# Linear attention within chunks: 32x32 blocks alone instead of 128-token score tiles

## The chip, the cores and the metric

One core of one Trainium2 chip. The metric is the device time of one execution, in microseconds (us); the kernel before was run three times, and one more execution was profiled.

## The reference, cut to what matters

The program is two networks one after the other, two layers each; the second one's layers hold the part that is changed. There, 512 tokens (256 of a context, 256 latent) are mixed by three mixers side by side: a gated linear attention with 6 heads (keys of 32, values of 64), a short convolution and a neighbourhood attention. The linear attention runs over the tokens in both directions, in chunks. In one direction, with decays accumulated into `q_dec` and `k_inv`:

```python
a = jnp.einsum('bnihk,bnjhk->bnhij', q_dec, k_inv)      # scores, within a chunk
a = jnp.where(causal, a, 0.0)
o_intra = jnp.einsum('bnhij,bnjhv->bnihv', a, v)
def step(s, xs):
    qd, ke, vv, dec = xs
    o = jnp.einsum('bihk,bhkv->bihv', qd, s)            # from the state before the chunk
    s = s * dec[..., None] + jnp.einsum('bjhk,bjhv->bhkv', ke, vv)
    return s, o
```

The two directions are added, each head is normalised by the root of its mean square, and the result is multiplied by a gate. All is fp32. The kernel takes chunks of 32 tokens (`GC`).

## The kernel before

The large products (`mtile`, `tokmajor`, `wtile`) form the main line: weights come in units of 128x1024, are split by ScalarE and VectorE into a high and a low part (`unit`), and each product is three matmuls of 128x128 against 256 to 512 columns (`mm3`, L388 to L390). The mixers are generators. The main line hands out a budget at each `tick`, also within a product (`inner`), and a generator spends what it yields; `until` runs the generators without any main product until one has finished. A scheduler then settles each engine's order when the program is built: it may take a main matmul of later program order ahead of one whose operands are not there. Inside `manual_schedule(engines={PE})` TensorE's instructions keep their order.

In PSUM, three banks (`mm`) belong to the main line, one (`ada`) to the modulation, and four (`ax`) to all else: the generators `gla` (linear attention) and `na` (neighbourhood attention) share these four.

`gla` prepares `Q[a]` and `K[a]` for a = 0 (forward, four heads), 1 (backward, four heads) and 2 (the last two heads, both directions); 32 partitions are one head. It then runs the chain of states `U` over the chunks (32x32 matmuls `ax<-bigA,bigD`), and then its last loop, one step for each 128 tokens: four steps in the first layer, two in the second. A step has for each r of four heads

- three matmuls of the scores, 32 rows by 128 columns of K against 128 columns of Q (`ax<-slG,slG`): the scores of 128 tokens with 128 tokens, of which only the four 32x32 blocks on the diagonal count;
- two masked copies and a multiplication on VectorE (L1595, L1596, L405), which write `AT[r]`, zero outside the blocks;
- two matmuls of `AT[r]`, 128x128, with 64 columns of values (`ax<-bigA,AT`), and up to twelve 32x32 matmuls of `Q2` with the state `U` (`ax<-gU,gq`), all added up in one bank, in a fixed order;
- a copy of this bank into `ot` by ScalarE.

The step ends with an addition on VectorE, a square on ScalarE, sums on VectorE, a power on GpSimd (`grr`, L519), a scaling on VectorE, three transposes on TensorE (L1644) and the product with the gate. After the first layer's short convolution `until` waits for `gla`; the next products of the main line are the queries and keys of the neighbourhood attention (`nqk(1)`, `nqk(2)`).

Of the kernel before, what the change touches and what calls it, by code (L numbers as in the profile page):

```python
# [10 lines left out]
U32 = mybir.dt.uint32  # L11
AF = mybir.ActivationFunctionType
ALU = mybir.AluOpType
# [26 lines left out]
ADA_MIX = range(16, 40)  # L40
MIX_PACE = 1.8
LAG = 2
GY = 300
GZ = 1500
SQP = (False, True)
GACT = True
# [14 lines left out]
GC = 32  # L61
# [34 lines left out]
def head_cols(base, heads):  # L96
# [3 lines left out]
C_VAL, C_GLU, C_GATE, P_IN, P_GATE, Q, K, V, A_GATE, QI, KI, WI = (  # L100
    0, 256, 512, 768, 1024, 1280, 1792, 2304, 2816, 3328, 3584, 3648)
# [178 lines left out]
def consts2():  # L280
    p = np.arange(128)
    f = p % 16
    inv = (np.float32(10000.0) ** (-np.arange(8, dtype=np.float32) / np.float32(8))).astype(np.float32)
    t = np.arange(T)
    pos = np.where((f < 8)[:, None], (t // 64)[None, :], (t % 64)[None, :]).astype(np.float32)
    ang = pos * inv[f % 8][:, None]
    sign = np.where(p % 32 < 16, -1.0, 1.0).astype(np.float32)[:, None]
    c = GC
    nch = 128 // c
    mats = []  # L290
    for back in range(2):
        m = np.zeros((128, 128 + 2 * nch))
        for i in range(128):
            c0 = i // c * c
            if not back:
                mid = c0 + c // 2 - 1
                m[mid + 1 : i + 1, i] = 1
                m[i + 1 : mid + 1, i] = -1
            else:
                mid = c0 + c // 2  # L300
                m[i:mid, i] = 1
                m[mid:i, i] = -1
        for k in range(nch):
            m[k * c : k * c + c // 2, 128 + 2 * k] = 1
            m[k * c + c // 2 : k * c + c, 129 + 2 * k] = 1
        mats.append(m / 16.0)
    j, i = np.arange(128)[:, None], np.arange(128)[None, :]
    same = j // c == i // c
    mf, mb, mbs = same & (j <= i), same & (j >= i), same & (j > i)
    sgn = np.where(p < 64, 1.0, -1.0)[:, None]  # L310
    qsc = np.where(p < 64, 32.0**-0.5, 1.0)[:, None]
    return np.concatenate(
        [np.cos(ang), np.sin(ang) * sign] + mats + [mf, mf, mb, mbs, 1.0 + np.eye(128), sgn, qsc], 1).astype(np.float32)


def consts0():
# [36 lines left out]
class Prog:  # L353
# [775 lines left out]
    def block2(s):  # L1129
        nc, A = s.nc, s.A  # L1130
        with ExitStack() as c:
            s.tmp = c.enter_context(s.tc.tile_pool(name="b2", bufs=1))
            c2 = s.t([128, A["c2"].shape[1]], "c2")
            nc.scalar.dma_start(c2, A["c2"])
            nch = 128 // GC
            w = 128 + 2 * nch
            s.cos, s.sin = c2[:, 0:256], c2[:, 256:512]
            s.gm = [c2[:, 512 + i * w : 512 + (i + 1) * w] for i in range(2)]
            o = 512 + 2 * w
            s.gmask, s.gdiag = c2[:, o : o + 512].bitcast(U32), c2[:, o + 512 : o + 640]  # L1140
            s.sgn, s.qsc = c2[:, o + 640 : o + 641], c2[:, o + 641 : o + 642]
            s.AT = [s.t([128, 256], f"AT{r}") for r in range(4)]
            for r in range(4):
                nc.gpsimd.memset(s.AT[r], 0.0)
            for i in range(DEPTH):
                s.layer2(i)

            R = s.spread(s.rstd_cols(s.st["ps"][:, 0:2], 2, 1.0 / D), 2)
            for k in range(KT):
                y = s.x2[:, k, T:]  # L1150
                s.stt(y, y, s.sp2[0]["fin"][:, k : k + 1], R[:, :T], ALU.mult, ALU.mult)
                if k % 2:
                    q = nc.sync if k % 4 == 1 else nc.scalar
                    q.dma_start(s.out[:, k - 1 : k + 1], s.x2[:, k - 1 : k + 1, T:])
# [306 lines left out]
    def gla(s, i, P, gw, v, glr, qk, both, c0, st8):  # L1461
        nc = s.nc
        mx = s.mx
        nch = 128 // GC
        NC = 4 * nch
# [4 lines left out]
        ps = s.bank()  # L1470
# [4 lines left out]
        for t in range(4):  # L1475
            ps = s.bank()
# [11 lines left out]
        Q = [s.sl("G") for _ in range(3)]  # L1488
        K = [s.sl("G") for _ in range(3)]
        w = 128 + 2 * nch  # L1490
        Dp = []
        for a, (d, off, dup) in enumerate([(0, 0, False), (1, 192, False), (0, 128, True), (1, 320, True)]):
            H = s.t([128, 4, 2 * nch], "gH", 2, pool=mx)
            for tp in ((0, 2) if d == 0 else (0, 2)):
                ps = s.bank()
                for t in (tp, tp + 1):
                    o = slice((t - tp) * w, (t - tp + 1) * w)
# [7 lines left out]
                c = slice(tp * 128, tp * 128 + 256)  # L1505
# [10 lines left out]
                else:  # L1516
                    x = s.t([128, T], "gx", 2, pool=mx)
                    s.a(vw(x), pv[:, :, 0:128], AF.Exp, scale=s.sgn)
                    o = slice(d * 64, d * 64 + 64)
# [27 lines left out]
            yield 0  # L1547

        U = s.t([128, 3, NC, 64], "gU", 1, pool=mx)
        fw = list(range(NC))  # L1550
        bw = list(range(NC // 2))[::-1] + list(range(NC // 2, NC))[::-1]
        sel = [(0, 0, slice(0, 128)), (2, 0, slice(0, 64)), (1, 1, slice(0, 128)), (2, 1, slice(64, 128))]
# [26 lines left out]
        st8["chain"] = True  # L1579
        while "r" not in st8:  # L1580
            yield None
        first = {0: 0, 1: NC // 2 - 1}
        out = s.big([128, 3, 512], "B")
        for t in tts:
            tc = slice(t * 128, t * 128 + 128)

            for r in range(4):
                ps = s.bank()
                rows = slice(r * 32, r * 32 + 32)
                for o, a in enumerate((0, 2, 1)):  # L1590
                    s.mm(ps[:, o * 128 : o * 128 + 128], K[a][rows, tc], Q[a][rows, tc])

                m0 = 0 if r < 2 else 128
                A2 = s.AT[r]
                nc.vector.copy_predicated(A2, s.gmask[:, m0 : m0 + 256], ps[:, :256])  # L1595
                nc.vector.copy_predicated(A2[:, 0:128], s.gmask[:, 384:512], ps[:, 256:384])  # L1596
                s.tt(A2[:, 0:128], A2[:, 0:128], s.gdiag, ALU.mult)
                yield 460

            Q2 = []  # L1600
            ch = slice(t * nch, t * nch + nch)
            for a in range(3):
                q2 = s.t([128, 128], "gq2", 3, pool=mx)
                for d, pr in ([(a, slice(0, 128))] if a < 2 else [(0, slice(0, 64)), (1, slice(64, 128))]):
                    Da = Dp[a] if a < 2 else Dp[2 + d]
                    f0 = first[d]
                    s.tt(q2[pr].rearrange("p (c x) -> p c x", x=GC),
                         Q[a][pr, tc].rearrange("p (c x) -> p c x", x=GC),
                         Da[pr, ch].unsqueeze(2).to_broadcast([pr.stop - pr.start, nch, GC]), ALU.mult)
                Q2.append(q2)  # L1610
            yield 600
            ot = s.sl("O", (128, 2, 4, 64))
            for r in range(4):
                with s.tc.manual_schedule(engines={mybir.EngineType.PE}):
                    ps = s.bank()
                    rows = slice(r * 32, r * 32 + 32)
                    h2 = 4 + r % 2
                    ops = []
                    ops.append((ps[:, 0:64], s.AT[r][:, 0:128], v[:, t, r * 64 : r * 64 + 64]))
                    ops.append((ps[:, 64:128], s.AT[r][:, 128:256], v[:, t, h2 * 64 : h2 * 64 + 64]))  # L1620
                    for a, d, col in [(0, 0, 0), (1, 1, 0), (2, 0 if r < 2 else 1, 64)]:
                        for c in range(nch):
                            ck = t * nch + c
                            pc = slice(c * GC, c * GC + GC)
                            if ck != first[d]:
                                ops.append((ps[pc, col : col + 64], Q2[a][rows, pc], U[rows, a, ck]))
                    for q, (o_, l, rh) in enumerate(ops):
                        s.mm(o_, l, rh, q == 0, q == len(ops) - 1, skip_group_check=True)
                s.a(ot[:, :, r], ps[:, :128].rearrange("p (c d) -> p c d", c=2), AF.Copy)
                if GY:  # L1630
                    yield GY
            s.tt(ot[:, 1, 0:2], ot[:, 1, 0:2], ot[:, 1, 2:4], ALU.add)
            of = ot.rearrange("p a b d -> p (a b d)")[:, 0:384]
            o3 = of.rearrange("p (h d) -> p h d", d=64)
            sq = s.sl("O", (128, 384))
            s.a(sq, of, AF.Square)
            ss = s.t([128, 6], "gss", 2, pool=mx)
            nc.vector.tensor_reduce(ss, sq.rearrange("p (h d) -> p h d", d=64), AX.X, ALU.add)
            yield 700
            rr = s.rstd_cols(ss, 6, 1.0 / 64, "gr")  # L1640
            s.tt(o3, o3, rr.unsqueeze(2).to_broadcast([128, 6, 64]), ALU.mult)
            ps = s.bank()
            for j in range(3):
                nc.tensor.transpose(ps[:, j * 128 : j * 128 + 128], of[:, j * 128 : j * 128 + 128], s.ident)  # L1644
            s.stt(out[:, :, tc], ps[:, :384].rearrange("p (j t) -> p j t", j=3), P["glag"], st8["r"][:, :, tc],
                  ALU.mult, ALU.mult)
            yield GZ
# [127 lines left out]
```

## Time and profile before

| | us |
|---|---|
| three runs | 1440.94, 1443.52, 1445.94 (median 1443.52) |
| profiled execution | 1444.92 |
| its span | 1443.1 |

In the profile PE is TensorE's matmuls, PEld its weight loads, DVE VectorE, ACT ScalarE, POOL GpSimd, SP the queue that starts most transfers. A row of instructions names line, engine, operation, what is written from what, partitions x elements, and how many (x). A matmul's form begins with rows*columns of its stationary operand. An fp32 matmul leaves two records, a matmul of the split main line one. Matmuls overlap, so the distance from start to start tells more than the length of one; the last number of a granted clock is a share of 2.4 GHz.

### The profile page before, as it was taken

The page shows a single profiled execution, that of the slowest core. Times are in us where ns is not written, and L with a number is a line of the kernel's source. Part 1 is how long each engine was busy: PE and PEld are TensorE (multiplying, and loading weights), DVE is VectorE, ACT ScalarE, POOL GpSimd, SP SyncE. Part 2 cuts the span into 40 slices and gives each one's busy share as a digit, 9 for nine tenths or more (in the row PEclk, how much of TensorE's full clock was granted, in tenths as well). Part 3 has the DMA queues.
Part 4 walks back from the last instruction along what each step waited for, and adds up shares of the span by engine and source line. Part 5 has one row for each costly group of instructions (what it writes and reads, how often), then busy time and mean ns, then how long its engine had stood idle before and what let it go on. Part 6 is the DMA issues. An engine that isn't in the chain of part 4 may idle for free.

```text
span 1443.1 us, 25346 instructions
## 1 busy us (share of the span) xinstructions
PE 1388.4 (96%) x9914; PEld 1188.0 (82%) x9914; DVE 1134.6 (79%) x2430; ACT 671.9 (47%) x1234; POOL 68.4 (5%) x92
## 2 busy tenths in 40 slices
PE   8999899998999999998999999999899999999997
PEld 7878899788978777678888888888788887999997
DVE  6998679997879666897788877888678556798794
ACT  4446555465753241545443312443145346565562
POOL 0000000000200001003000000001200000100001
PEclk9999899998999998999999999999999999999998
DMA  7973356334543432332444564557732232366662
GB/s 263 330 250 118 103 170 201 125 104 130 194 148 116 132 100 73 117 114 89 133 144 132 160 191 146 174 177 251 229 115 89 89 97 88 116 212 197 183 198 74
DMA packets 63903, 219.03 MB, mean 152 GB/s; under 512 B 7270, under 2 KB 12328, under 8 KB 63528
## 3 DMA queue, kind: packets, MB, share of 16 engines
q1 hardware_dynamic: 58368, 209.22, 45.8%
q10 hardware_dynamic: 5416, 8.20, 1.7%
q8 instruction: 78, 1.28, 0.4%
q14 instruction: 41, 0.34, 0.1%
HBM read 216.34 MB, written 1.05 MB: 151 GB/s over the span
## 4 chain that ended last, share of the span: by engine, by line
PE 73%; DVE 11%; issue 6%; DMA 4%; ACT 3%; POOL 2%; ACTq 0%; POOLq 0%; DVEq 0%; SPq 0%
PE mm L388 20%; PE mm L389 20%; PE mm L390 19%; PE ax L385 9%; DVE hl L449 3%; DMA wada<-in_wadaT_dram 2%; PE mm L385 1%; DMA raw<-in_units_dram 1%; PE ax L1728 1%; PE ada L385 1%; POOL sqa L537 1%; DVE xx L396 1%; DVE wada L683 1%; DMA crow<-in_crow_dram 1%; ACT hl L441 1%
## 5 line engine op out<-in xcount | busy, mean ns | idle before, releaser
L388 PE MATMUL mm<-xx,hl 128*128 128x256 f32 (+1 forms) x1720 | 557.5, 326 | 5.5 <-ACT xx L414 2.0
L390 PE MATMUL mm<-xx,hl 128*128 128x256 f32 (+1 forms) x1720 | 547.1, 319 | 1.6 <-DVE hl L449 1.5
L389 PE MATMUL mm<-xx,hl 128*128 128x256 f32 (+1 forms) x1720 | 547.6, 319 | 0.0
L441 ACT ACTIVATE hl<-raw 128x1024 fp32r<-128x1024 f32 x286 | 301.3, 1055 | 186.8 <-PE mm L390 152.4
L449 DVE TENSOR_TENSOR hl<-raw,hl 128x1024 fp32r<-128x1024 f32 x286 | 348.9, 1221 | 49.3 <-ACT hl L441 47.6
L388 PEld LDWEIGHTS mm<-xx,hl 128*128 128x128 f32 x1720 | 325.6, 190 | 51.8 <-issue 17.9
L390 PEld LDWEIGHTS mm<-xx,hl 128*128 128x128 f32 x1720 | 325.9, 190 | 30.6 <-DVE hl L449 3.2
L389 PEld LDWEIGHTS mm<-xx,hl 128*128 128x128 f32 x1720 | 326.5, 190 | 28.4 <-issue 4.9
L396 DVE SCALAR_TENSOR_TENSOR y<-mm,sp,y 128x255 f32<-128x255 f32 (+1 forms) x184 | 109.0, 595 | 30.9 <-ACT y L409 29.6
L389 PE MATMUL mm<-hid,hl 128*128 128x256 f32 (+1 forms) x374 | 124.2, 332 | 0.0
L388 PE MATMUL mm<-hid,hl 128*128 128x256 f32 (+1 forms) x374 | 124.2, 332 | 0.0
L390 PE MATMUL mm<-hid,hl 128*128 128x256 f32 (+1 forms) x374 | 124.1, 332 | 0.0
L683 DVE CUSTOM_DVE_ANT_0 wada<-wada,crow,sp 128x1024 f32<-128x1024 f32 x80 | 102.9, 1292 | 13.6 <-DMA wada<-in_wadaT_dram 13.2
L409 ACT ACTIVATE y<-mm,sp 128x256 f32<-128x256 f32 (+1 forms) x92 | 60.5, 658 | 97.9 <-PE mm L390 97.8
L390 PEld LDWEIGHTS mm<-hid,hl 128*128 128x128 f32 x374 | 71.9, 192 | 7.1
L388 PEld LDWEIGHTS mm<-hid,hl 128*128 128x128 f32 x374 | 71.8, 192 | 7.1
L389 PEld LDWEIGHTS mm<-hid,hl 128*128 128x128 f32 x374 | 71.8, 192 | 7.1
L389 PE MATMUL mm<-hl,xx 128*128 128x416 f32 (+3 forms) x192 | 65.9, 346 | 2.5 <-DVE hl L449 2.5
L396 DVE SCALAR_TENSOR_TENSOR x<-mm,mod,x 128x256 f32<-128x256 f32 x96 | 43.6, 479 | 30.2 <-PE mm L390 30.1
L537 POOL TENSOR_TENSOR sqa<-sqa,sq 128x256 f32<-128x256 f32 x36 | 35.3, 987 | 675.7 <-ACT sq L409 674.8
L388 PE MATMUL mm<-hl,xx 128*128 128x416 f32 (+3 forms) x192 | 65.9, 349 | 0.2 <-ACT hl L441 0.2
L390 PE MATMUL mm<-hl,xx 128*128 128x416 f32 (+3 forms) x192 | 65.6, 344 | 0.0
(278 smaller groups left out, 1691.0 us busy)
## 6 DMA issues: line engine op xcount, KB each, us to landing
raw<-in_units_dram SPq DMA_DIRECT2D x296, 512.0 KB, 3.8
wada<-in_wadaT_dram SPq DMA_DIRECT2D x80, 512.0 KB, 3.5
wada<-in_wada_dram SPq DMA_DIRECT2D x16, 512.0 KB, 6.2
nab<-in_nab_dram ACTq DMA_DIRECT2D x12, 192.0 KB, 3.4
crow<-in_crow_dram SPq DMA_DIRECT2D x2, 1024.0 KB, 7.4
x<-in_xT_dram SPq DMA_DIRECT2D x4, 256.0 KB, 5.9
x<-in_ctxT_dram ACTq DMA_DIRECT2D x1, 1024.0 KB, 11.9
c<-in_c_dram ACTq DMA_DIRECT2D x1, 928.0 KB, 5.9
```

The costliest lines, as they stand in the source:

```text
L385: return s.nc.tensor.matmul(out, lhsT, rhs, start=start, stop=stop, **kw)
L388: s.nc.tensor.matmul(out, l[0], r[0], start=start, stop=False)
L389: s.nc.tensor.matmul(out, l[0], r[1], start=False, stop=False)
L390: s.nc.tensor.matmul(out, l[1], r[0], start=False, stop=stop)
L396: s.nc.vector.scalar_tensor_tensor(out, a, sc, b, op0, op1)
L409: s.nc.scalar.activation(out, in_, func, bias=bias, scale=scale)
L441: a = nc.scalar.activation(hl[:, 0], raw, AF.Copy)
L449: b = nc.vector.tensor_sub(hl[:, 1], raw, hl[:, 0].bitcast(F32))
L537: (eng or s.nc.vector).tensor_tensor(st["acc"], st["acc"], sq, ALU.add)
L683: s.pin(nc.vector.tensor_tensor_reduce(out=w, in0=w, in1=c[:, j], scale=1.0, scalar=bias[:, m : m + 1], op0=ALU.mult, op1=ALU.add, accum_o ...
L1728: nc.tensor.transpose(pt[:, kt * 128 : kt * 128 + 128], L[j][:, kt * 128 : kt * 128 + 128], s.ident)
```

## The change

The scores are computed by 32x32 blocks alone, each into its 32 partitions and 32 columns of a bank, two heads at once in two banks, TensorE's order kept. ScalarE copies each head's 96 columns into `pk`, and after all four heads VectorE masks them at once into `AT[t % 2]`, which now has 4 x 64 columns. Scores times values are 32x32 matmuls too, per chunk, into one bank `px` for all heads of the step, which VectorE adds to `of` after the last head; the state matmuls keep a bank for each head. They now run over the first chunk of each direction too, whose state is cleared to zero by GpSimd. The yields of a step change (`GY` and others), and the masks among the constants shrink to 32 columns.

```diff
-GY = 300
+GY = 200
...
-            s.AT = [s.t([128, 256], f"AT{r}") for r in range(4)]
-            for r in range(4):
+            s.AT = [s.t([128, 4, 2 * GC], f"AT{r}") for r in range(2)]
+            for r in range(2):
                 nc.gpsimd.memset(s.AT[r], 0.0)
...
+        first = {0: 0, 1: NC // 2 - 1}
+        for a, d, pr in [(0, 0, slice(0, 128)), (1, 1, slice(0, 128)), (2, 0, slice(0, 64)), (2, 1, slice(64, 128))]:
+            nc.gpsimd.memset(U[pr, a, first[d]], 0.0)
...
-            for r in range(4):
-                ps = s.bank()
-                rows = slice(r * 32, r * 32 + 32)
-                for o, a in enumerate((0, 2, 1)):
-                    s.mm(ps[:, o * 128 : o * 128 + 128], K[a][rows, tc], Q[a][rows, tc])
-
-                m0 = 0 if r < 2 else 128
-                A2 = s.AT[r]
-                nc.vector.copy_predicated(A2, s.gmask[:, m0 : m0 + 256], ps[:, :256])
-                nc.vector.copy_predicated(A2[:, 0:128], s.gmask[:, 384:512], ps[:, 256:384])
-                s.tt(A2[:, 0:128], A2[:, 0:128], s.gdiag, ALU.mult)
-                yield 460
+            pk = s.t([128, 4, 3 * GC], "gpk", 1, pool=mx)
+            for r0 in (0, 2):
+                bk = [s.bank(), s.bank()]
+                with s.tc.manual_schedule(engines={mybir.EngineType.PE}):
+                    for o, a in enumerate((0, 2, 1)):
+                        for c in range(nch):
+                            for r in (r0, r0 + 1):
+                                rows = slice(r * 32, r * 32 + 32)
+                                pc = slice(t * 128 + c * GC, t * 128 + c * GC + GC)
+                                s.mm(bk[r - r0][c * GC : c * GC + GC, o * GC : o * GC + GC], K[a][rows, pc], Q[a][rows, pc])
+                for r in (r0, r0 + 1):
+                    s.a(pk[:, r], bk[r - r0][:, : 3 * GC], AF.Copy)
+                yield 300
+
+            A2 = s.AT[t % 2]
+            nc.vector.copy_predicated(A2, s.gmask, pk[:, :, 0 : 2 * GC])
+            nc.vector.copy_predicated(A2[:, :, 0:GC], s.gback, pk[:, :, 2 * GC :])
+            s.tt(A2[:, :, 0:GC], A2[:, :, 0:GC], s.gdiag.unsqueeze(1).to_broadcast([128, 4, GC]), ALU.mult)
+            yield 500
...
             ot = s.sl("O", (128, 2, 4, 64))
+            px = s.bank()
             for r in range(4):
+                ps = s.bank()
+                rows = slice(r * 32, r * 32 + 32)
+                h2 = 4 + r % 2
                 with s.tc.manual_schedule(engines={mybir.EngineType.PE}):
-                    ps = s.bank()
-                    rows = slice(r * 32, r * 32 + 32)
-                    h2 = 4 + r % 2
-                    ops = []
-                    ops.append((ps[:, 0:64], s.AT[r][:, 0:128], v[:, t, r * 64 : r * 64 + 64]))
-                    ops.append((ps[:, 64:128], s.AT[r][:, 128:256], v[:, t, h2 * 64 : h2 * 64 + 64]))
-                    for a, d, col in [(0, 0, 0), (1, 1, 0), (2, 0 if r < 2 else 1, 64)]:
+                    for q, (a, col) in enumerate([(0, 0), (None, r), (1, 0), (None, h2), (2, 64)]):
                         for c in range(nch):
-                            ck = t * nch + c
                             pc = slice(c * GC, c * GC + GC)
-                            if ck != first[d]:
-                                ops.append((ps[pc, col : col + 64], Q2[a][rows, pc], U[rows, a, ck]))
-                    for q, (o_, l, rh) in enumerate(ops):
-                        s.mm(o_, l, rh, q == 0, q == len(ops) - 1, skip_group_check=True)
+                            if a is None:
+
+                                x = int(col > 3)
+                                s.mm(px[pc, col * 64 : col * 64 + 64], A2[pc, r, x * GC : x * GC + GC],
+                                     v[pc, t, col * 64 : col * 64 + 64], r == 0 and not x, r == 3 and x == 1,
+                                     skip_group_check=True)
+                            else:
+                                s.mm(ps[pc, col : col + 64], Q2[a][rows, pc], U[rows, a, t * nch + c], a == 0, a == 2,
+                                     skip_group_check=True)
                 s.a(ot[:, :, r], ps[:, :128].rearrange("p (c d) -> p c d", c=2), AF.Copy)
...
             of = ot.rearrange("p a b d -> p (a b d)")[:, 0:384]
+            s.tt(of, of, px[:, :384], ALU.add)
```

## Rows read from the trace of the kernel before

**Rows 1.** Page: busy time, share of the span and instructions of each engine.

```profile
...
PE 1388.4 (96%) x9914; PEld 1188.0 (82%) x9914; DVE 1134.6 (79%) x2430; ACT 671.9 (47%) x1234; POOL 68.4 (5%) x92
...
```

**Rows 2.** Windows of 10 us: length, busy time of each engine, PE clock.

```profile
...
470.00:480.00 10.00, 10.00 (x76) 7.49 (x61) 9.68 (x27) 1.98 (x3) 0.00 (x0) 1.00 0.48 148
...
1170.00:1180.00 10.00, 10.00 (x168) 9.11 (x167) 1.95 (x4) 3.35 (x8) 0.00 (x0) 1.00 0.26 65
...
```

**Rows 3.** Waits of PE, 470-580 and 1138-1190: total us, times, longest.

```profile
...
PE ax L1644 <- DVE slO L405: 2.7, 3, 1.0
...
PE ax L1644 <- DVE slO L405: 3.2, 2, 1.7
...
```

**Rows 4.** Chain of work that ended last, 470-580: start, us, what.

```profile
...
473.12 0.24 PE mm L390
...
477.20 1.19 PE ax L385 x12
...
479.99 0.86 PE ax L385 x6
480.85 0.43 PE mm L388
...
531.97 0.85 PE ax L385 x24
...
549.62 3.21 PE ax L385 x84
...
```

**Rows 5.** Timeline, PE: the first and last of 18 stretches of scores.

```profile
...
474.68 0.93 PE L385 MATMUL ax<-slG,slG 32*128 32x128 f32 x6
...
1167.02 0.93 PE L385 MATMUL ax<-slG,slG 32*128 32x128 f32 x6
...
```

**Rows 6.** Timeline, PE: scores times values, the first and last of 24.

```profile
...
482.28 0.55 PE L385 MATMUL ax<-bigA,AT 128*128 128x64 f32 x4
...
1177.26 0.66 PE L385 MATMUL ax<-bigA,AT 128*128 128x64 f32 x4
...
```

**Rows 7.** Timeline, PE, 440 to 456: blocks of the chain of states.

```profile
...
442.79 0.56 PE L385 MATMUL ax<-bigA,bigD 32*32 32x64 f32 x24
...
446.17 0.40 PE L388 MATMUL mm<-xx,hl 128*128 128x512 f32 x1
446.49 0.84 PE L385 MATMUL ax<-bigA,bigD 32*32 32x64 f32 x48
447.27 0.50 PE L389 MATMUL mm<-xx,hl 128*128 128x512 f32 x1
447.60 0.40 PE L390 MATMUL mm<-xx,hl 128*128 128x512 f32 x1
...
```

**Rows 8.** Groups by line and form, PE: the last loop's state matmuls.

```profile
...
L385 PE MATMUL ax<-gU,gq 32*32 32x64 f32 x552 | 14.1, 234 | 0.0
...
```

**Rows 9.** Instructions on the tile AT, DVE: ns, least, median and most.

```profile
...
L1595 DVE COPY_PREDICATED AT<-c,ax x24: 430/441/450, 477.4 to 1168.0; 128x256 f32<-128x256 uint32 x24
L1596 DVE COPY_PREDICATED AT<-c,ax x24: 289/296/306, 478.9 to 1169.5; 128x128 f32<-128x128 uint32 x24
L405 DVE TENSOR_TENSOR AT<-AT,c x24: 274/286/294, 480.3 to 1169.8; 128x128 f32<-128x128 f32 x24
...
```

**Rows 10.** Timeline, ACT and DVE: a head's copy, the step's scaling.

```profile
...
554.88 0.28 ACT L409 ACTIVATE slO<-ax 128x128 f32<-128x128 f32 x1 [1.70 <-PE ax L385]
...
560.23 0.56 DVE L405 TENSOR_TENSOR slO<-slO,grr 128x384 f32<-128x384 f32 x1 [1.21 <-POOL grr L519]
...
```

**Rows 11.** Timeline, PE: main matmuls around the first layer's last step.

```profile
...
559.75 0.39 PE L390 MATMUL mm<-xx,hl 128*128 128x512 f32 x1
...
564.04 0.50 PE L388 MATMUL mm<-xx,hl 128*128 128x512 f32 x1
...
```

**Rows 12.** Windows of 2 us, columns as in the second group.

```profile
...
564.00:566.00 2.00, 2.00 (x21) 1.69 (x23) 2.00 (x10) 0.30 (x1) 0.00 (x0) 0.70 0.79 248
...
578.00:580.00 2.00, 2.00 (x11) 1.45 (x9) 0.62 (x1) 0.90 (x2) 0.00 (x0) 0.89 0.00 0
...
```

More of the change, by code (lines that the diff above doesn't have):

```diff
@@ L306, in consts2 @@
         mats.append(m / 16.0)
-    j, i = np.arange(128)[:, None], np.arange(128)[None, :]
-    same = j // c == i // c
-    mf, mb, mbs = same & (j <= i), same & (j >= i), same & (j > i)
+    j, i = np.arange(128)[:, None] % c, np.arange(c)[None, :]
+    mf, mb, mbs = j <= i, j >= i, j > i
     sgn = np.where(p < 64, 1.0, -1.0)[:, None]
@@ L312, in consts2 @@
     return np.concatenate(
-        [np.cos(ang), np.sin(ang) * sign] + mats + [mf, mf, mb, mbs, 1.0 + np.eye(128), sgn, qsc], 1).astype(np.float32)
+        [np.cos(ang), np.sin(ang) * sign] + mats + [mf, mf, mf, mf, mf, mb, mf, mb] + [mbs] * 4 + [1.0 + (j == i), sgn, qsc], 1).astype(np.float32)
 def consts0():
@@ L1139, in block2 @@
             o = 512 + 2 * w
-            s.gmask, s.gdiag = c2[:, o : o + 512].bitcast(U32), c2[:, o + 512 : o + 640]
-            s.sgn, s.qsc = c2[:, o + 640 : o + 641], c2[:, o + 641 : o + 642]
-            s.AT = [s.t([128, 256], f"AT{r}") for r in range(4)]
-            for r in range(4):
+            m = 8 * GC
+            s.gmask = c2[:, o : o + m].bitcast(U32).rearrange("p (r x) -> p r x", r=4)
+            s.gback = c2[:, o + m : o + m + 4 * GC].bitcast(U32).rearrange("p (r x) -> p r x", r=4)
+            o += m + 4 * GC
+            s.gdiag = c2[:, o : o + GC]
+            s.sgn, s.qsc = c2[:, o + GC : o + GC + 1], c2[:, o + GC + 1 : o + GC + 2]
+            s.AT = [s.t([128, 4, 2 * GC], f"AT{r}") for r in range(2)]
+            for r in range(2):
                 nc.gpsimd.memset(s.AT[r], 0.0)
@@ L1581, in gla @@
             yield None
-        first = {0: 0, 1: NC // 2 - 1}
         out = s.big([128, 3, 512], "B")
@@ L1605, in gla @@
                     Da = Dp[a] if a < 2 else Dp[2 + d]
-                    f0 = first[d]
                     s.tt(q2[pr].rearrange("p (c x) -> p c x", x=GC),
```

## The prediction

> **What bounds the kernel now.** I began with the page's busy line: TensorE (PE) has work for 96% of the span and VectorE (DVE) for 79%, so a microsecond of PE work that goes away can be worth a microsecond, if it goes away where PE is the limit [rows 1]. The stretch that the change touches lies inside the mixers of block 2, once per layer. The windows show PE busy for all ten microseconds there, at full clock, with DVE at 9.7 in the first layer's window and at 1.95 in the second layer's [rows 2]: PE is full whether DVE is full or nearly idle. The waits say what is left over: PE stood still behind other engines mostly at one place, the transposes at the end of a step of 128 tokens, 2.7 us in three waits and 3.2 us in two [rows 3]. So the main line's matmuls fill nearly every hole, and what the linear attention costs is what its matmuls take from them. I therefore price PE first.
>
> **PE, scores, before.** A step makes 12 score matmuls of 32x128 against 128 columns, 24 records (each fp32 matmul leaves two), 144 records in the 6 steps. The chain of waits has 6 of them in 0.86 us and 12 in 1.19 us, and the main matmul behind them takes 0.43 us where an undisturbed one takes 0.24 [rows 4]. So a stretch costs 0.33 / 6 = 0.055 us for each record, and (0.86 - 0.33) + 0.19 = 0.72 us for breaking into the main line. The timeline has 18 such stretches [rows 5]: 18 x 0.72 + 144 x 0.055 = 13.0 + 7.9 = 20.9 us.
>
> **PE, values and state, before.** Three heads in a row, with their score-times-value matmuls on the full array and their 32x32 state matmuls, take 3.21 us [rows 4], 1.07 each; I take 1.05, since one alone has the same price (0.85 + 0.19, by the same view). 24 of them: 25.2 us. They stand in 16 stretches, in 8 places one directly behind another [rows 6]. Together 46.1 us at full clock.
>
> **PE, after.** Everything is 32x32: 48 matmuls of scores a step (96 records in 2 pinned groups of 48), and per head 12 state matmuls and 8 of scores times values (40 records). The trace has just such blocks, the 32x32 matmuls of the state chain. 24 records last 0.56 us and 48 last 0.84 us, that is 0.28 / 24 = 11.7 ns a record; the 48 push two main matmuls 1.10 us apart, where they otherwise follow by 0.24 [rows 4], and the next one by 0.33, which is 0.09 late [rows 7]. So 48 records cost 1.10 - 0.24 + 0.09 = 0.95 us, and n records 0.39 + 0.0117 n. Scores: 12 x 0.95 = 11.4. Values: 16 x 0.86 for a head that breaks in, 8 x 0.47 for one directly behind another: 13.8 + 3.8 = 17.6. Together 29.0, a gain of 17.1 us. From both sides: were a record free, 28 x 0.39 = 10.9 us would be left and the gain were 35.2; the dearest row is the group of state matmuls, 14.1 us busy over 552 records, 25.5 ns each [rows 8], which makes 1536 x 0.0255 + 10.9 = 50.1 (12 x 48 + 24 x 40 = 1536 records), a loss of 4.0. I take 11.7, since the new order alternates between tiles of two row groups as the chain's blocks do, and its score matmuls have half the columns.
>
> Here a page of the Trainium skill speaks against the change. "TensorEngine Tiling (Array Packing)", section Instruction Overhead, gives each matmul an overhead of about 60 cycles, so that a short one costs as much as one of 60 columns; at 2.4 GHz this is an estimate of 25 ns, and 1536 records at 25 ns would make the new stretches dearer than the old. The chain's blocks do not agree, at 11.7 ns a record; the group of state matmuls would.
>
> **DVE and ScalarE (ACT).** DVE loses four times 441 + 296 + 286 ns a step and keeps one set of these [rows 9], which is 3.07 us less; the new addition of the values' bank, 128x384, is nearest to the multiplication of the same shape at 0.56 us [rows 10]. Net -2.5 us a step, -15 us in all, but DVE does not set the time here, so I count it as nothing. If PE did not cover it, it would be a gain of up to 15 us instead of PE's, not beside it. ACT gains four copies of 128x96 a step, nearest 0.28 us [rows 10]: 1.1 us a step, 6.7 in all. They are hidden in ACT's idle time; queued behind them in ACT's order are the splits of weights, and if the main line ran out of weights they would cost those 6.7 us.
>
> **New waits.** The addition stands in the tail from the last head to the transposes (copy, additions, square, sums, power on GpSimd, scaling), where PE already waits [rows 3]. It makes the tail 0.56 us longer; 0 to 3.4 us in six steps, as main matmuls fill it or not. I take 1.5. A first head now waits for four copies and one set of three DVE operations, 4 x 0.28 + 1.02 = 2.1 us, instead of its own set alone, 1.02. Main matmuls stand behind it in program order, and PE takes them first, as it does now; nothing counted. The bank of the values is held through all four heads, of four banks shared with the neighbourhood attention, so fewer heads can be in flight; that is in the rival below. The four clearings of first states go to GpSimd, whose queue holds nothing but the step's power there, and the constants' load shrinks: nothing.
>
> **The order.** A step's yields sum to 5,840 units before and 4,700 after, so main tiles and steps interleave closer together and the steps end earlier; the main line has the next query and key tiles to go on with. No gain counted, but it bears on the clock. In the first layer's last step, PE's last main matmul starts at 559.75 and the next at 564.04, with score matmuls between [rows 11]; then the granted clock is at its lower level, 1.2 GHz, from about 564.8 to 578.4 us (0.70 in one window, 0.89 in the last) [rows 12]. PE is busy throughout, so these 13.6 us cost 6.8 us.
>
> **The sum.** -17.1 + 1.5 = -15.6 us. The profiled execution took 1444.9 us (its span is 1443.1), which makes 1429.3; the median of the three runs is 1.4 us lower, so 1427.9. I say 1428. About 0.3%, 4.3 us, is what a measurement of this kernel can tell from no change.
>
> **Rivals.** First, the fall of the clock goes away, because the stretch without main matmuls gets shorter. For it: the score records of a step are done sooner, and the copies and masks then leave some 2 us in which only main matmuls can run. Against it: the wait for GpSimd's power in the same place stays. Time: 1428 - 6.8 = 1421. Second, the waits eat the gain: if the 2.1 us before each step's first head were bare, or heads queued for banks, 6 x 2.1 = 12.6 us are lost, 1441, no change that can be told. For it: the last step of the first layer has few main matmuls between its heads. Against it: the main line's next tiles are there, and PE waited only 5.9 us in both stretches. Third, on the other side: 32x32 records at the pace of the dearest group, 25.5 ns. Then the change costs 4.0 + 1.5 = 5.5 us: 1449. The point from which it decides is where 1536 p + 10.9 + 1.5 reaches 46.1, p = 21.9 ns. For it: that group's own mean. Against it: that mean includes the change of tiling before and after only 24 records; blocks of 48 do better. The skill's section named above is this same rival by its 25 ns. More falls of the clock would also cost, 6.8 us each of this length; it takes more than two to turn the sign.
>
> **Chances.** The forecast (PE gains, clock as before) 0.42; the clock's fall gone 0.26; waits eat most of it, 1434 to 1444, 0.20; slower, by the pace of records or by more falls of the clock, 0.12. Of the third case somewhat over half is within 0.3%. So faster 0.76, same 0.12, slower 0.12. The range that leaves out no more than two in ten goes from a little below the second case, 1416, into the third, 1440; that of the likeliest case alone is 1424 to 1434.
>
> **What would show it.** Right: score groups of 48 records of 32x32 that push main matmuls about 1.1 us apart, heads of 40 records at about 0.9 us; DVE's copies under the mask 12 instead of 48; PE's records up by about 744 and the windows of both stretches still full of PE. Wrong: a pitch of 20 ns or more in these blocks; PE's waits for ACT's copies or for banks in place of main matmuls; a granted clock of 0.5 in windows where it was 1.0.

## The result, and the profile after

The kernel after takes 1425.64 us (median of 4 runs, 1419.99 to 1429.48), the kernel before 1444.73 beside it: a ratio of 0.9866 [0.9835, 0.9898], 1.3% faster. The profiled execution is the fastest of the four, 1419.99 us with a span of 1418.2.

The page's busy line of after, which answers to [rows 1], and the windows that answer to [rows 2]:

```profile
...
PE 1363.1 (96%) x10658; PEld 1167.0 (82%) x10658; DVE 1126.9 (79%) x2382; ACT 675.8 (48%) x1258; POOL 69.1 (5%) x98
...
```

```profile
...
470.00:480.00 10.00, 9.63 (x282) 7.38 (x280) 7.31 (x16) 3.14 (x9) 0.00 (x0) 1.00 0.63 211
...
1115.00:1125.00 10.00, 10.00 (x299) 8.69 (x298) 4.71 (x13) 3.63 (x11) 0.00 (x0) 1.00 0.33 106
...
```

PE has 744 records more and 25 us less to do; its share stays 96%. PE is busy for 9.63 and 10.00 of the 10 us of these windows, with 282 and 299 records where the windows of before had 76 and 168.

A score group in after's timeline of PE, which answers to [rows 5], and a head of 40 records, of which the first and the last rows stand:

```profile
...
533.37 0.40 PE L389 MATMUL mm<-xx,hl 128*128 128x512 f32 x1
...
534.31 0.39 PE L390 MATMUL mm<-xx,hl 128*128 128x512 f32 x1
534.63 0.62 PE L385 MATMUL ax<-slG,slG 32*32 32x32 f32 x48
535.18 0.50 PE L388 MATMUL mm<-xx,hl 128*128 128x512 f32 x1
535.52 0.39 PE L389 MATMUL mm<-xx,hl 128*128 128x512 f32 x1
...
```

```profile
...
510.41 0.39 PE L388 MATMUL mm<-xx,hl 128*128 128x512 f32 x1
510.72 0.26 PE L385 MATMUL ax<-gU,gq 32*32 32x64 f32 x4
...
511.18 0.29 PE L385 MATMUL ax<-gU,gq 32*32 32x64 f32 x3
511.41 0.50 PE L389 MATMUL mm<-xx,hl 128*128 128x512 f32 x1
511.75 0.39 PE L390 MATMUL mm<-xx,hl 128*128 128x512 f32 x1
...
```

The row of 48 score records at 534.63 lasts 0.62 us with the end of its last one (0.19); from the first start to the last it is 0.43, so a record starts every 9 ns. It pushes two main matmuls 0.87 us apart, where 0.235 is undisturbed (533.37 to 534.31 in four distances), and the next follows 0.34 behind: 0.87 - 0.235 + 0.105 = 0.74 us. The head takes 1.00 - 0.235 + 0.105 = 0.87 us, and its 40 records start within 0.54 us, one every 13.5 ns.

I reckoned every such stretch of scores, values and state in both traces in this way, with time at half clock counted half. Before: scores 20.6, values and state 25.1, together 45.7 us. After: 8.5 and 17.7, together 26.2. The gain on PE is 19.5 us, where 17.1 was forecast.

Waits of PE in after, at 470 to 580 and 1110 to 1160 (total us, times, longest), which answer to [rows 3]:

```profile
...
PE ax L1660 <- DVE slO L405: 5.5, 3, 2.8
...
PE ax L1660 <- DVE slO L405: 3.3, 2, 1.8
PE ax L385 <- ACT slO L409: 1.0, 1, 1.0
```

The longest of them, 2.76 us, in after's timeline: PE has no main matmul behind the one at 546.42 while GpSimd's power runs, where in before main matmuls started up to 559.75 [rows 11].

```profile
...
546.42 0.39 PE L390 MATMUL mm<-xx,hl 128*128 128x512 f32 x1
546.50 2.33 POOL L519 TENSOR_TENSOR grr<-grm,mhalf 128x6 f32<-128x6 f32 x1 [22.35 <-DVE grm L515]
...
549.57 0.52 PE L1660 MATMUL ax<-c,slO 128*128 128x128 f32 x3 [2.76 <-DVE slO L405]
...
```

DVE's instructions on the tile AT in after (ns: least, median, most), which answer to [rows 9]: 6 of a kind, not 24.

```profile
...
L1609 DVE COPY_PREDICATED AT<-c,gpk x6: 442/448/453, 475.1 to 1134.4; 128x256 f32<-128x256 uint32 x6
L1610 DVE COPY_PREDICATED AT<-c,gpk x6: 300/304/307, 475.6 to 1136.9; 128x128 f32<-128x128 uint32 x6
L405 DVE TENSOR_TENSOR AT<-AT,c x6: 281/291/293, 475.9 to 1137.5; 128x128 f32<-128x128 f32 x6
...
```

The clock at the first layer's last step of after, in windows of 2 us as in [rows 12]:

```profile
...
550.00:552.00 2.00, 1.86 (x106) 1.59 (x106) 2.00 (x6) 1.21 (x5) 0.00 (x0) 0.88 0.27 102
552.00:554.00 2.00, 2.00 (x6) 1.58 (x5) 1.51 (x4) 0.06 (x1) 0.00 (x0) 0.50 0.22 53
554.00:556.00 2.00, 2.00 (x61) 1.43 (x62) 0.00 (x0) 0.00 (x0) 0.00 (x0) 0.76 0.54 209
...
```

The fall is still there, but loses 2 x (0.12 + 0.50 + 0.24) = 1.7 us instead of 6.8. Another fall is missing in this execution: before's at 404 to 414 us, granted 0.66, and after's at the same work, granted 1.00.

```profile
...
404.00:414.00 10.00, 10.00 (x28) 6.78 (x29) 3.51 (x10) 5.62 (x6) 0.00 (x0) 0.66 0.16 65
...
```

```profile
...
401.00:411.00 10.00, 10.00 (x37) 6.30 (x37) 3.55 (x9) 5.33 (x8) 0.00 (x0) 1.00 0.41 152
...
```

That work lies before the chain of states and all changed matmuls, but PE's order differs between the two traces from 382 us on. The three profiles with the old scores (before, and two kernels of the experiments: values only, and before with new yields) have a fall there, and of the eleven with the new scores only that of "heads in pairs" has. So it is open whether the 3.4 us that it gave belong to the change. One profile holds the falls of one execution and is no measure of the clock's part. Each run lists its span and mean granted clock; I split the span of every run in two: span times clock is its time at full clock, the rest is what the clock cost. This is bookkeeping: it counts work of the other engines and waits at the lower level as if they too had run at half speed. All times below in us; the last two columns are means over the runs of a kernel, and the medians are times of the whole execution. Each ratio is to the runs of before made beside that kernel, of which the 29 in the first line are the largest set (two others are 1412.5 and 1413.3 at full clock, and the four beside after list no clock):

| kernel | runs | median | ratio to before, 95% | at full clock | lost to the clock |
|---|---|---|---|---|---|
| before | 29 | 1442.22 | | 1412.2 | 28.7 |
| after | 4 | 1425.64 | 0.9866 [0.9835, 0.9898] | 1396.3 | 27.1 |
| values only | 12 | 1438.17 | 0.997 [0.9955, 0.9984] | 1404.6 | 30.9 |
| scores only | 12 | 1448.67 | 1.0039 [1.0016, 1.0062] | 1405.4 | 41.1 |
| VectorE's work put back | 5 | 1425.07 | 0.9885 [0.9866, 0.9904] | 1396.5 | 26.5 |
| before, new yields | 12 | 1441.11 | 0.9984 [0.9963, 1.0004] | 1408.9 | 30.2 |
| after, old yields | 12 | 1436.17 | 0.9955 [0.9937, 0.9974] | 1402.8 | 31.2 |
| after, old yield of heads | 4 | 1429.57 | 0.991 [0.9892, 0.9927] | 1396.3 | 31.4 |
| after, shorter yields | 6 | 1430.16 | 0.9899 [0.9874, 0.9925] | 1396.8 | 30.5 |
| transposes later | 6 | 1426.1 | 0.9874 [0.9851, 0.9898] | 1396.6 | 27.5 |
| no addition of values | 6 | 1429.36 | 0.9906 [0.9883, 0.9928] | 1398.1 | 30.0 |
| heads in pairs | 4 | 1429.69 | 0.9914 [0.9887, 0.994] | 1400.1 | 28.2 |
| pairs, scores joined | 4 | 1427.56 | 0.9896 [0.9879, 0.9914] | 1396.0 | 29.9 |
| states, then values | 4 | 1434.3 | 0.9942 [0.9927, 0.9957] | 1398.4 | 34.0 |

Runs of one kernel differ by 1.7 to 3.5 us (standard deviation) at full clock and by 1.4 to 4.6 in the loss. At full clock the change is worth 1412.2 - 1396.3 = 15.9 us, give or take some 3 with four runs of after; the clock adds 1.6, which these few runs cannot tell from nothing.

### The profile page after: what moved, and what is told of

It is laid out like the page before. It is cut to its first block, busy times and chain, and to the rows that moved or that the text cites. A ratio compares the mean times of both kernels' runs of the same rounds, so it can differ in the third digit from the quotient of the medians.

```text
span 1418.2 us, 26810 instructions
## 1 busy us (share of the span) xinstructions
PE 1363.1 (96%) x10658; PEld 1167.0 (82%) x10658; DVE 1126.9 (79%) x2382; ACT 675.8 (48%) x1258; POOL 69.1 (5%) x98
## 4 chain that ended last, share of the span: by engine, by line
PE 71%; DVE 14%; issue 6%; DMA 4%; ACT 3%; POOL 2%; ACTq 0%; POOLq 0%; DVEq 0%
PE mm L388 20%; PE mm L389 19%; PE mm L390 19%; PE ax L385 8%; DVE hl L449 3%; DMA wada<-in_wadaT_dram 2%; PE mm L385 1%; DVE wada L683 1%; DMA raw<-in_units_dram 1%; PE ada L385 1%; DVE gU L396 1%; PE ax L1744 1%; ACT hl L441 1%; DVE x L396 1%; POOL sqa L537 1%
## 5 line engine op out<-in xcount | busy, mean ns | idle before, releaser
L396 DVE SCALAR_TENSOR_TENSOR y<-mm,sp,y 128x255 f32<-128x255 f32 (+1 forms) x184 | 109.1, 595 | 31.4 <-ACT y L409 30.1
L396 DVE SCALAR_TENSOR_TENSOR x<-mm,mod,x 128x256 f32<-128x256 f32 x96 | 43.7, 479 | 31.4 <-PE mm L390 31.4
```

What stands on the lines that cost most here:

```text
L396: s.nc.vector.scalar_tensor_tensor(out, a, sc, b, op0, op1)
```

## The experiments

The theory: TensorE's time in the new stretches is the gain. Its rivals: VectorE's relief is the gain; the new yields, that is the order, are; the clock is.

**1. One half of the change alone**, both with the new yields. Values and state as after, scores as before, with the new yields; and the scores as after, values as before (there the masks are twelve operations of 32 partitions a step, into a full 128x128 tile for all four heads).

```diff
+                    for q, (a, col) in enumerate([(0, 0), (None, r), (1, 0), (None, h2), (2, 64)]):
...
+                                s.mm(px[pc, col * 64 : col * 64 + 64], s.AT[r][pc, x * 128 + c * GC : x * 128 + c * GC + GC],
```

> The kernel before with the values' half of the change alone: scores and masks as before (32x128 matmuls, VectorE masks per head into the full 128x128 tile), scores times values as 32x32 blocks into a bank of their own, which VectorE adds at the end of a step; the yields of a step sum to 4,700 as in the changed kernel. Theory 1 (TensorE's time is the gain): in the two traces the stretches of values and state matmuls add up to 29.5 us before and 17.7 after, so about 12 us less than before, near 1433, ratio 0.992. Rival (relief of VectorE is the gain): VectorE loses nothing here and gets six additions of 0.54 us, so 0 to 3 us more than before, 1445 to 1448. Rival (closer pacing by the yields is the gain): all of the 19 us, 1426.

```diff
-            s.AT = [s.t([128, 4, 2 * GC], f"AT{r}") for r in range(2)]
+            s.ATf = s.t([128, 4, 256], "AT")
...
+                nc.vector.copy_predicated(A4[pc, :, :, pc], xj(s.gmask[pc]), xj(pk[pc, :, 0 : 2 * GC]))
...
+                    ops.append((ps[:, 0:64], s.ATf[:, r, 0:128], v[:, t, r * 64 : r * 64 + 64]))
```

> The changed kernel with the scores' half alone: 32x32 score blocks, ScalarE's copies, but the masks go by 12 VectorE operations a step on 32 partitions each into a full 128x128 tile for each head, which costs VectorE about the time of the kernel before, and scores times values run as 128x128 matmuls in the state's bank, as before. Theory 1: the stretches of score matmuls add up to 20.6 us before and 8.8 after, so about 12 us less than before, near 1433, ratio 0.992; the sum of the two halves should come near the whole change's 19 us or somewhat over it. Rival (VectorE): no gain, 1443 to 1447. Rival (pacing): 1426.

At full clock the halves give 1412.2 - 1404.6 = 7.6 and 1412.2 - 1405.4 = 6.8 us, together 14.4 of the 15.9. The yields are in both; with their 3.3 us (experiment 3) counted once it is 11.1, so the halves do not add up to the whole. Each half had been expected to give 12 us; both missed that. By its time the second half alone is 0.4% slower than before. Its profile shows much of why: PE's waits at 465 to 585 us, and a window of 14 us.

```profile
...
PE ax L385 <- DVE AT L405: 5.2, 3, 3.0
...
```

```profile
...
479.00:493.00 14.00, 14.00 (x119) 11.37 (x119) 3.63 (x9) 2.01 (x6) 1.33 (x1) 0.51 0.14 42
...
```

PE waits 3.0 us bare for the masks, then runs the heads' matmuls, and the clock falls to 0.51 for the next 14 us, 14 x 0.49 = 6.9 us lost there; over its runs the clock costs 12.4 us more than in before. With 2.5 us in the second layer PE waits 7.7 us for the masks in this kernel, which also takes from its gain at full clock. So the second rival of the prediction, a bare wait in front of the first head, is real in this kernel, and the clock makes it dearer than the wait itself. In after the same wait is 0.4 us.

**2. VectorE's work put back**: after, with the masks done three times more into a spare tile.

```diff
+            for _ in range(3):
+                nc.vector.copy_predicated(s.spare, s.gmask, pk[:, :, 0 : 2 * GC])
+                nc.vector.copy_predicated(s.spare[:, :, 0:GC], s.gback, pk[:, :, 2 * GC :])
+                s.tt(s.spare[:, :, 0:GC], s.spare[:, :, 0:GC], s.gdiag.unsqueeze(1).to_broadcast([128, 4, GC]), ALU.mult)
```

> The changed kernel with three more sets of the masked copies and the multiplication a step, written into a spare tile that nobody reads: VectorE has again the 3.07 us a step that the change took from it. Theory 1: VectorE is not the limit, so 1426 to 1429. Rival (VectorE): the gain goes back by most of 18 us, 1440 or more.

1396.5 us at full clock against after's 1396.3: VectorE's relief is worth nothing here. That rival falls.

**3. The yields.** Before with after's yields; after with before's; after with those of the heads alone put back; after with still shorter ones.

```diff
-GY = 300
+GY = 200
...
-                yield 460
+                yield 275
```

> The kernel before with nothing but the shorter yields (275 for each head's scores in place of 460, 200 in place of 300), so that a step sums to 4,700. The runs so far, each as its mean span times its mean granted clock (time at full clock): before 1412, whole change 1396, whole change with the old yields 1403. Theory 1 (the blocks are the gain, yields only move work): no change, 1439 to 1445, at full clock 1412. Rival (the yields are worth some 6 to 7 us by themselves, and each half contained that): 1434 to 1437, at full clock 1405 to 1406. Third (yields help only with the new blocks): 1442, at full clock 1412, with the stretches as in the kernel before.

```diff
-GY = 200
+GY = 300
...
-                yield 300
+                yield 660
...
-            yield 500
+            yield 520
```

> The changed kernel with the yields of a step summing to 5,840 again (scores 660 + 660 + 520, heads 300). Theory 1: yields only move work along the main line, so 1426 give or take 4. Rival (pacing): at least half of the gain is lost, 1436 or more.

```diff
-GY = 200
+GY = 300
```

> After, with the yield behind each head at 300 units as in the kernel before; the yields of the scores as after. The run with all old yields lost about 10 us. If the yield between heads is its cause (heads broken into one by one by main matmuls, a longer step): 1432 to 1438. If the yields of the scores are: within 0.3% of after, 1422 to 1430.

```diff
-GY = 200
+GY = 100
...
-                yield 300
+                yield 150
...
-            yield 500
+            yield 300
```

> The changed kernel with yields shorter still: a step sums to 3,800 (scores 150 + 150 + 300, heads 100). Rival (pacing): another 3 to 6 us less, 1420 to 1423. Theory 1: 1426 give or take 3, with more done in one piece and perhaps more time at the low clock.

By themselves the new yields do not move the time of the kernel before by what can be told (0.9984 [0.9963, 1.0004]), but at full clock it is 3.3 us shorter, between the values expected (1412, or 1405 to 1406). The blocks by themselves, with the old yields, give 1412.2 - 1402.8 = 9.4 us at full clock. So 9.4 and 3.3 of the 15.9 are the blocks' and the yields' own, and 3.2 come only with both, which is no more than twice its standard error of 1.6. The time of after with the old yields, 1436, is what had been expected if pacing were half of the gain or more. The heads' yield alone costs nothing at full clock, so it is those of the scores; shorter ones bring nothing more, and the 3 to 6 us expected of them for pacing did not come. Where did the 6.5 us go that the old yields cost after? PE's waits at the transposes are 4.7 and 4.1 us in that profile, as long as in after. The last feed-forward products tell a part of it. First a window of after and of after with old yields, then the first and the last of 13 matmuls in a row of each:

```profile
...
1265.00:1280.00 15.00, 15.00 (x135) 15.00 (x134) 14.18 (x26) 10.58 (x18) 0.00 (x0) 1.00 0.61 196
...
```

```profile
...
1265.00:1280.00 15.00, 15.00 (x130) 15.00 (x129) 14.58 (x26) 10.34 (x18) 0.00 (x0) 1.00 0.73 214
...
```

```profile
...
1261.75 0.28 PE L389 MATMUL mm<-xx,hl 128*128 128x256 f32 x1
...
1263.11 0.28 PE L389 MATMUL mm<-xx,hl 128*128 128x256 f32 x1
...
```

```profile
...
1271.75 0.28 PE L389 MATMUL mm<-xx,hl 128*128 128x256 f32 x1
...
1273.16 0.28 PE L389 MATMUL mm<-xx,hl 128*128 128x256 f32 x1
...
```

The same matmuls of 256 columns run at the same granted clock with PE full in both, and the distance from start to start is 1.36 / 12 = 113 ns in the one and 1.41 / 12 = 118 in the other; the window's counts, 135 and 130, include those that began before it. After has 135 in each such window from 1235 to 1295 us, but 128 and 129 in the two from 1300 to 1330; after with old yields has 127 to 130 in each window of 15 us from 1250 to 1375. Of the 8.4 us at full clock by which this profile is longer than after's, some 3 are this slower pace and some 3 longer gaps between main matmuls; the stretches take 1 to 2. So most of the loss is not in the changed code's own matmuls.

The pace does not explain the mean, however. The profiles of "no addition of values", "states, then values", "transposes later" and "heads in pairs" have 129 or 130 in this window too, before has 134, and "transposes later" takes the same 1396.6 us at full clock as after over its runs. With one profile for each kernel it stays open whether the pace belongs to a kernel or to an execution, what sets it, and what the old yields' 6.5 us are.

**4. The tail of a step.** After without the addition of the values' bank (the part of the output from within the chunk is left out), and after with the transposes put further behind the scaling.

```diff
-            s.tt(of, of, px[:, :384], ALU.add)
```

> The changed kernel without VectorE's addition of the values' bank at the end of a step: the part of the output from within the chunk is left out, TensorE's work stays. The forecast took 1.5 us (0 to 3.4) as the price of the longer tail. Theory 1: 0 to 3.4 us less than the changed kernel, 1422 to 1426. Rival (the tail's waits eat much of the gain): 6 us less or more, 1420 or less.

```diff
-GZ = 1500
+GZ = 700
...
             rr = s.rstd_cols(ss, 6, 1.0 / 64, "gr")
+            yield 800
```

> The changed kernel with a yield of 800 between GpSimd's power and the scaling with the transposes, taken from the yield at the end of the step (1,500 to 700). In the trace of the changed kernel PE waits 5.5 us in three and 3.3 us in two places before these transposes. If those waits come from the transposes' place in PE's order, 3 to 6 us less, 1420 to 1423; if main matmuls cannot fill the place, 1426.

Neither gains; without the addition the time, 1429.4, lies above both values expected for it. PE's wait at the transposes of the first layer without the addition (465 to 585 us):

```profile
...
PE ax L1659 <- DVE slO L405: 5.7, 3, 3.0
...
```

It is 5.7 us in three waits, against 5.5 with the addition; with the transposes later it is 5.3. So the longer wait of after is not the addition's, though that is where I had put a price, and a yield there does not bring main matmuls in front of the transposes.

**5. The shape of the stretches.** Two heads' 80 records in one pinned block, alternating between their row groups; the same with both score groups directly behind each other; and after with each head's state matmuls first, then its values.

```diff
+            for r0 in (0, 2):
+                bk = [s.bank(), s.bank()]
                 with s.tc.manual_schedule(engines={mybir.EngineType.PE}):
+                    for q in range(5):
                         for c in range(nch):
+                            for r in (r0, r0 + 1):
...
+                yield 2 * GY
```

> After, with two heads' 80 records in one pinned block, alternating between the two heads' row groups and banks, and the two yields given behind it. Theory 1 (a stretch costs a fixed part for breaking into the main line plus its records): the heads' 24 stretches become 12, each pair costs about 1.33 instead of 2 x 0.86 us where both broke in, -2 to -5 us, and if alternation brings the 9 ns a record of the score groups in place of 13.5, another -4: 1417 to 1424, the heads' stretches at full clock from 17.7 to 10 to 14 us. Rival (order and waits decide what the freed time is worth): the stretches shrink but the time stays within 0.3% of after, 1422 to 1430.

```diff
-                yield 300
+                if r0:
+                    yield 600
```

> As heads in pairs, and the two score groups of a step are given directly one behind the other, with one yield of 600 behind both. Theory 1: six stretches of 96 records at about 1.1 us instead of twelve at 0.745, another -2 us: 1415 to 1422. Rival: the second group needs the last two of the four shared banks, so it waits for ScalarE's copies or for the neighbourhood attention, and the step starts later: no gain against heads in pairs, or 2 to 6 us slower.

```diff
-                    for q, (a, col) in enumerate([(0, 0), (None, r), (1, 0), (None, h2), (2, 64)]):
+                    for q, (a, col) in enumerate([(0, 0), (1, 0), (2, 64), (None, r), (None, h2)]):
```

> After, with each head's 12 state matmuls first and its 8 score-times-value matmuls behind them, instead of the two kinds interleaved by four. If the interleaving (a change of row group at every fourth matmul) sets the 13.5 ns a record of the heads' stretches, those stretches get shorter, to 0.40 to 0.48 us a head, -1 to -3 us in all; if 64 columns a matmul set it, they stay at 0.54; if staying within one row group is dear, they get longer, 0.6 to 0.8. Time: within 0.3% of after in the first two cases, 1422 to 1430; 2 to 6 us slower in the third.

A pair in the first of these, in its timeline of PE (first and last rows):

```profile
...
515.49 0.28 PE L385 MATMUL ax<-gU,gq 32*32 32x64 f32 x8
...
516.27 0.31 PE L385 MATMUL ax<-gU,gq 32*32 32x64 f32 x6
516.51 0.50 PE L389 MATMUL mm<-xx,hl 128*128 128x512 f32 x1
...
```

80 records start within 0.88 us, 11.0 ns each; two heads one behind the other in after take 0.98, 12.2 ns. Alternating the row groups (the state matmuls do so at every matmul, the values change row group with the chunk) does quicken the records, but by 0.1 us a pair, about 1 us in all, and the time does not follow: 1400.1 and 1396.0 us at full clock, 1396.3 in after. The break-ins that I hoped to save were mostly gone already: in after's trace 11 of 24 heads stand directly behind another one, in 13 stretches, and the pairs make 12. Both expectations of a gain missed. With the states first a head keeps 0.53 to 0.55 us, so the order of the two kinds does not set the 13.5 ns. Pairs alternating as above bring it to 11.0; the score groups, which alternate two row groups at every matmul and have half the columns, to 9. With the states first the median is 1434.3 us, above the 1422 to 1430 expected for an unchanged pace: a mere change of order, with the same stretches, moved the whole execution by 0.6%. At full clock that is 2.1 us and the clock cost 6.9 more, by four runs of each, too few to tell the two parts apart.

## Why the prediction was right, point by point

**TensorE bounds the kernel**: right. The gain is there at full clock with VectorE's work put back, 1412.2 - 1396.5 = 15.7 us, and the blocks alone, with the old yields, bring 9.4 of it.

**Before, 46.1 us**: by the same reckoning of all stretches 45.7. **After, 29.0 us**: 26.2. The heads' 17.6 measured 17.7. The scores' 11.4 measured 8.5. I priced them by blocks of 64 columns [rows 7], with 11.7 ns a record and 0.39 us for breaking in; groups of 48 and of 96 records (0.74 and 1.19 us) give 0.45 / 48 = 9.3 ns a record and 0.30 us. That makes 576 x 2.4 ns = 1.4 us and 12 x 0.09 = 1.1 us of the 2.9. The reason given for 11.7, that the chain's blocks alternate between two row groups, is wrong: in the kernel's loop over `sel` 12 matmuls in a row keep their row group, and only the column group changes. The price held for the heads, whose state matmuls keep their row group as well; the scores, which do alternate and have half the columns, are cheaper.

**The pace of the rival on the other side, 25.5 ns**, was not what happened, and its row misleads: the same view of after gives the state matmuls 15.4 us of busy time for 576 records.

```profile
...
L385 PE MATMUL ax<-gU,gq 32*32 32x64 f32 x576 | 15.4, 223 | 0.0
...
L385 PE MATMUL ax<-bigA,AT 32*32 32x64 f32 x384 | 12.6, 222 | 0.4 <-DVE AT L405 0.4
...
```

These are 26.7 and 32.8 ns a record, 28.0 us together, more than the 17.7 us that the stretches cost PE: records of 0.22 us overlap with those of the other form, and the busy time of each counts the shared time. Start to start was the price. The Trainium skill's "TensorEngine Tiling (Array Packing)", Instruction Overhead, about 60 cycles a matmul, does not hold for the scores: a score matmul leaves two records and so takes 18 ns in all, less than the 25 ns estimated from that rule even for one. The prediction set those 25 ns against each of the 1536 records; as the price of a matmul, of which there are 768, they make an estimate of 19.2 us, and the heads' matmuls, at 2 x 13.5 = 27 ns, lie a little over 25, those of the pairs of experiment 5, at 22, a little under. The Trainium skill's "TensorEngine Tiling (Array Packing)" says in its section Key Properties that different tiles load and multiply in parallel, and that a change of tiling mode drains the engine; the 9 ns and the 0.30 us of a break-in agree with that.

**The tail, +1.5 us**: not shown. PE's waits at the transposes in both stretches grew from 5.9 to 8.8 us (2.9 more), with 1.0 and 0.4 us at two other places; but they stay when the addition goes, and the time does not fall. The longest has no main matmul during GpSimd's power; why PE had none left there is open.

**The order, "no gain counted"**: the weakest step. At full clock the yields are worth 3.3 us in the kernel before and 6.5 with the new blocks. The forecast had no term for this.

**The clock, unchanged**: right in the mean (28.7 and 27.1 us lost), while the profiled execution alone would have spoken for the first rival: 29.6 us lost in before's, 22.0 in after's. The fall that this rival named did get shorter there, 1.7 instead of 6.8 us lost, but over the runs the whole loss is nearly the same. The profile's 24.9 us of shorter span are 19.5 from the stretches and 7.6 from the clock, and 2.2 were given back. Where is not settled: the waits at the transposes are longer, but PE's idle time as a whole, span less busy time, is 54.7 us before and 55.1 after.

**The sum**, -15.6 forecast, is -15.9 at full clock, and 1428 us forecast is 1425.64; that it agrees so closely is luck, since the parts do not: the scores were priced 2.9 us too dear, waits at the transposes grew by 2.9 where 1.5 stood, and while the old yields stand the blocks bring only 9.4 us, where the stretches of that profile, 27.5 us by the same reckoning, are 18.2 shorter than before's. Why the freed time arrives in full only with the new yields is not settled.

## What to carry to other kernels

Price short matmuls by the distance from start to start in a block of the same shape and mixture, never by a group's busy time divided by its count. Split each run's span by its granted clock before comparing variants within 1%: its loss went from 26.5 to 41.1 us between the kernels here, and one profile can hold a lucky one. Change yields or order only with several runs, since states first, then values, the same work in another order, moved the time by 0.6%.

## What the runs showed of the hardware that was not expected

- 32x32 fp32 records start every 9 ns with 32 columns in two alternating row groups, every 11.0 with 64 columns in pairs of heads whose state matmuls alternate between two row groups, every 13.3 to 13.7 with 64 columns in a head of one row group and its values.
- A stream of main matmuls of 256 columns runs at 113 or at 118 ns from start to start for tens of microseconds on end, at a granted clock of 1.00 and with PE full in both. Both paces occur in after's own trace (135 records in the window at 1265 to 1280, 128 in that at 1300 to 1315).
- After a bare wait of PE of 3.0 us the granted clock was 0.51 for 14 us, in which PE was busy throughout.
